# PSUM banks of an expert stage: gate and up sums in a ring of three, all transposes in another ring of three

## The chip, the cores and the metric

The kernel runs on one core of a Trainium2 chip. The metric is device time in microseconds for one execution. The median of three runs before the change is 2891.22 us (2885.97 to 2896.53).

## The reference

One layer of a hybrid block (chunked gating, grouped-query attention, a bidirectional gated recurrence, one output projection) is followed by a mixture of 32 experts. Each of the 2048 tokens, 1024 wide, takes two experts. For every block of an expert's rows the stage computes

```
return (jax.nn.silu(xb @ w1[e]) * (xb @ w3[e])) @ w2[e]
```

with w1 and w3 of 1024 x 512 and w2 of 512 x 1024, multiplies by the gate and adds the rows up by token. Everything is fp32.

## The kernel before

The change lies in the expert stage alone, the function `moe` (L1356 to L1602), which takes the last 830 us. Experts are ranked by their number of tokens, each rank has a fixed room (`CAPS`, L37), and the room is cut into blocks of 128 rows, the last one of 64 where the room is odd. That gives 47 blocks: 29 full ones and 18 half ones. The list `seq` takes turns between large, middle and small experts.

**Precision.** fp32 products are made of three matmuls. A value is split into a high part (fp32r, written by ScalarE) and a low part (the rest, written by VectorE), in `split`, whose two instructions have the lines L82 and L85 wherever it is called. The weights are split the same way by `split_next` (L1425 on ScalarE, L1426 on VectorE). `half16` (L1446, GpSimd) makes a 16-bit copy of the high part.

**Weights.** `pump` (L1410) loads one piece of 512 KB by SyncE into one of five staging tiles `wstage`; the piece is split, its staging tile comes free when L1426 has read it, and the next load is issued. Split pieces wait in rings of 15 (w1, w3) and 7 (w2). Where in the program a piece is split is fixed when the program is built: `need` forces the pieces of the next matmuls, and `ahead` adds one for every 5 units of matmul work if the ring has room.

**One turn.** All engines but SyncE run in program order, and turn i emits, in this order: the gather of the rows of block i+2; a quarter of `gate_up(i)`; `hidden(i-1)`; the scatter of block i-2; a second quarter of `gate_up(i)`; `rows(i+1)`; the rest of `gate_up(i)` with its epilogue; `down(i-1)`.

- `rows` (L1456) transposes the gathered rows of a block on TensorE, eight tiles of 128 columns into the PSUM tile `pxt`, and splits it in two pieces s = 0 and 1 of four tiles each: ScalarE copies the high part `xh` (L82), VectorE subtracts (L85).
- `gate_up` (L1508) adds x @ w1 in the PSUM tile `ph1` and x @ w3 in `ph3`. The first matmuls of a block write `ph1` (two in a full block, one in a half one), the next ones `ph3`, and so on in turns. The epilogue of a full block is SiLU of `ph1` on ScalarE (L1533) and the product with `ph3` on VectorE (L1534). A half block keeps its low products in the other 64 partitions, so ScalarE copies (L1526, L1527) and VectorE adds (L1528, L1529) before SiLU (L1530) and the product (L1531).
- `hidden` (L1473) transposes the product into `pat` and splits it; `down` (L1537) multiplies by w2 into `py`.

The PSUM pool `moep` has one buffer of every tile: `pxt` two banks, `pat` one, `ph1` and `ph3` one each, `py` two; seven of eight banks. A tile's next user waits for all readers of the last one.

Of the kernel before, what the change touches and what calls it, by code (L numbers as in the profile page):

```python
# [10 lines left out]
F32 = mybir.dt.float32  # L11
# [5 lines left out]
OP = mybir.AluOpType  # L17
# [4 lines left out]
P = 128  # L22
D = 1024
KT = D // P
# [50 lines left out]
class Kern:  # L75
# [1280 lines left out]
    def moe(self):  # L1356
        nc, tc, a = self.nc, self.tc, self.a
# [9 lines left out]
        with ExitStack() as es:  # L1367
            pool = es.enter_context(tc.tile_pool(name="moe", bufs=2, reuse_waits="tile"))
            ps = es.enter_context(tc.tile_pool(name="moep", bufs=1, space=PSUM, reuse_waits="tile"))
# [60 lines left out]
            def need(r, w, k):  # L1430
                while (r, w, k) not in W:
                    split_next()
                    clock[0] = max(clock[0] - self.PACE, -self.PACE)
                return W[r, w, k]
# [3 lines left out]
            def ahead(t):  # L1438

                clock[0] = min(clock[0] + t, 3 * self.PACE)  # L1440
                while clock[0] >= self.PACE and dq and free[kind(dq[0][0][1])] > 0:
                    split_next()
                    clock[0] -= self.PACE

            def half16(o, x):
                nc.gpsimd.tensor_scalar(o, x, -65504.0, 65504.0, op0=OP.max, op1=OP.min)  # L1446
# [9 lines left out]
            def rows(i):  # L1456

                n = 64 if half(*seq[i]) else P
                xg = XG.pop(i)
                pt = ps.tile([P, KT, n], F32, name="pxt")  # L1460
                for k in range(KT):
                    nc.tensor.transpose(pt[:, k], xg[:n, k * P:(k + 1) * P], self.ident[:n, :n])
                x = []
                for s in range(2):
                    h = pool.tile([P, 4, P], F32R, name="xh", bufs=4)
                    l = h[:, :, 64:] if n == 64 else pool.tile([P, 4, P], F32R, name="xl", bufs=4)
                    b = pool.tile([P, 4, P], F16, name="xb", bufs=4)
                    self.split(h[:, :, :n], l, pt[:, 4 * s:4 * s + 4])
                    half16(b[:, :, :n], h[:, :, :n])
                    x.append((h, l, b))  # L1470
                XT[i] = x

            def hidden(i):  # L1473

                n = 64 if half(*seq[i]) else P
                ac = AC.pop(i)
                pt = ps.tile([P, 4, n], F32, name="pat")
                for k in range(4):
                    nc.tensor.transpose(pt[:, k], ac[:n, k * P:(k + 1) * P], self.ident[:n, :n])
                h = pool.tile([P, 4, P], F32R, name="ah", bufs=1)  # L1480
                l = h[:, :, 64:] if n == 64 else pool.tile([P, 4, P], F32R, name="al", bufs=1)
                b = pool.tile([P, 4, P], F16, name="ab", bufs=1)
                self.split(h[:, :, :n], l, pt)
                half16(b[:, :, :n], h[:, :, :n])
                AT[i] = [(h, l, b)]

            def mm(i, out, x, ws, cs, last):


                small = half(*seq[i])  # L1490
                first = small and (cs[0] // 2) % 2 == 1
                for low in ((True, False) if first else (False, True)):
                    for m, c in enumerate(cs):
                        h, l, b = (v[:, c % 4] for v in x[c // 4])
                        for s in range(2):
                            w = ws[s][m][low]
                            if not low:
                                nc.tensor.matmul(out[s], h, w, start=(c == 0), stop=(first and c == last))  # L1498
                                if not small:
                                    nc.tensor.matmul(out[s], l, w, start=False, stop=False)  # L1500
                            elif small:
                                z = slice(64 * s, 64 * s + 64)
                                nc.tensor.matmul(out[s][z], b[:, :64], w, start=False, stop=False,
                                                 tile_position=(0, 64 * s))
                            else:
                                nc.tensor.matmul(out[s], b, w, start=False, stop=(c == last))

            def gate_up(i):  # L1508

                r, j = seq[i]  # L1510
                x = XT.pop(i)
                p1 = ps.tile([P, 512], F32, name="ph1")
                p3 = ps.tile([P, 512], F32, name="ph3")
                for kk in range(4):
                    pcs = [need(r, w, kk) for w in ("w1", "w3")]
                    ws = [[[v[:, k * 512:(k + 1) * 512] for v in pc] for k in range(2)] for pc in pcs]
                    mm(i, (p1, p3), x, ws, (2 * kk, 2 * kk + 1), KT - 1)
                    if j == nb(r) - 1:
                        free["w13"] += 2
                    ahead(6.5 if half(r, j) else 12)  # L1520
                    yield
                sg = pool.tile([P, 512], F32, name="sg", bufs=1)
                ac = AC[i] = pool.tile([P, 512], F32, name="ac", bufs=1)
                if half(r, j):
                    z = slice(0, 64)
                    nc.scalar.activation(sg[z], p1[64:], AF.Copy)  # L1526
                    nc.scalar.activation(ac[z], p3[64:], AF.Copy)  # L1527
                    nc.vector.tensor_tensor(sg[z], p1[z], sg[z], op=OP.add)  # L1528
                    nc.vector.tensor_tensor(ac[z], p3[z], ac[z], op=OP.add)  # L1529
                    nc.scalar.activation(sg[z], sg[z], AF.Silu, scale=1.0 / UP)  # L1530
                    nc.vector.scalar_tensor_tensor(ac[z], ac[z], 1.0 / UP, sg[z], op0=OP.mult, op1=OP.mult)  # L1531
                else:
                    nc.scalar.activation(sg, p1, AF.Silu, scale=1.0 / UP)  # L1533
                    nc.vector.scalar_tensor_tensor(ac, p3, 1.0 / UP, sg, op0=OP.mult, op1=OP.mult)  # L1534
                yield
# [37 lines left out]
            with tc.manual_schedule(engines=ENGINES):  # L1573
                for i in range(4):
                    fetch(i)
                for _ in range(self.STG):
                    pump()
                gather(0)
                gather(1)
                rows(0)  # L1580
                for i in range(N):
                    fetch(i + 4)
                    if i + 2 < N:
                        gather(i + 2)
                    g = gate_up(i)
                    next(g)
                    if i:
                        hidden(i - 1)

                    if i > 1:  # L1590
                        scatter(i - 2)
                    next(g)
                    if i + 1 < N:
                        rows(i + 1)
                    for _ in g:
                        pass
                    if i:
                        down(i - 1)
                hidden(N - 1)
                scatter(N - 2)  # L1600
                down(N - 1)
                scatter(N - 1)  # L1602
# [154 lines left out]
```

## Time and profile before

| What | Value |
|---|---|
| Median of three runs | 2891.22 us |
| The profiled execution: its own time, its span | 2883.17 us, 2881.5 us |
| Busy over the span: TensorE, VectorE, GpSimd, ScalarE | 2583.3, 2034.3, 1740.4, 1602.0 us |
| Moved by DMA in the whole program | 410.01 MB, mean 142 GB/s |
| Loads of expert weights | 384 of 512 KB each |

Times are microseconds from the span's start. PE is TensorE, ACT ScalarE, DVE VectorE, POOL GpSimd, SP SyncE. "[1.41 <-DVE xl L85]" behind an instruction in a timeline says that its engine was idle for 1.41 us before it and what ended that. Durations of matmuls overlap: they are pipelined, and the distance of their starts is the time that one takes.

### The profile page before, as it was taken

The numbers are of one execution on the slowest core, as the hardware profiler recorded it, in microseconds if no ns is written. First come the engines' busy times: TensorE is split into PE (matmuls) and PEld (weight loads), VectorE is DVE, ScalarE is ACT, GpSimd is POOL, SyncE is SP. The second block draws the span as 40 slices with busy tenths as digits, with TensorE's granted clock in tenths as the row PEclk, the third lists the DMA queues.
The fourth block names the chain that finished last, engine by engine and source line by source line (L and its number), as shares of the span: only waits on it lengthen the run. The fifth ranks groups of instructions, "written<-read, shape, count | busy, mean of one in ns | idle before, by whom it ended". The sixth has DMA issues, their size and how long they took to land. (4 is left out here: it accounts for less than half of the span.)

```text
span 2881.5 us, 39891 instructions
## 1 busy us (share of the span) xinstructions
PE 2583.3 (90%) x13276; PEld 1904.5 (66%) x13276; DVE 2034.3 (71%) x3049; ACT 1602.0 (56%) x2695; POOL 1740.4 (60%) x1374
## 2 busy tenths in 40 slices
PE   6888898679977999999999999899599999998886
PEld 3788887668865666666666676777366666654553
DVE  3787877674445667667777763778578888888886
ACT  3555554312223777777888774222366666666664
POOL 3335333547774778778888886555455765555553
PEclk9999999789997999999999999999699999999998
DMA  7221223233321111111110005442599999999996
GB/s 284 100 79 63 92 81 106 58 94 99 103 83 50 62 60 59 61 59 40 32 32 31 14 13 172 133 153 99 187 291 298 292 294 312 315 308 299 310 301 171
DMA packets 208688, 410.01 MB, mean 142 GB/s; under 512 B 27568, under 2 KB 82224, under 8 KB 208352
## 3 DMA queue, kind: packets, MB, share of 16 engines
q1 hardware_dynamic: 194976, 367.52, 37.7%
q0 software_dynamic: 13504, 39.93, 6.4%
q8 instruction: 105, 1.72, 0.2%
q14 instruction: 103, 0.84, 0.1%
HBM read 336.00 MB, written 71.37 MB: 141 GB/s over the span
## 5 line engine op out<-in xcount | busy, mean ns | idle before, releaser
L972 POOL TENSOR_TENSOR pl<-pf,ph 128x512 f16<-128x512 f32 x512 | 683.6, 1344 | 156.0 <-ACT ph L969 131.0
L909 DVE TENSOR_REDUCE mx<-pmx 128x1 f32<-128x512 f32 (+1 forms) x640 | 403.3, 635 | 206.8 <-PE pmx L907 199.9
L968 ACT ACTIVATE pf<-s 128x512 f32<-128x512 f32 x576 | 344.3, 598 | 178.5 <-PE s L965 162.4
L1426 DVE SCALAR_TENSOR_TENSOR w13l<-wstage,w13h 128x1024 f16<-128x1024 f32 x256 | 317.8, 1277 | 40.2 <-ACT w13h L1425 37.0
L969 ACT ACTIVATE ph<-s 128x512 fp32r<-128x512 f32 x576 | 342.4, 594 | 0.0
L1498 PE MATMUL ph<-w13h,xh 128*128 128x512 f32 x752 | 291.1, 433 | 48.4 <-DVE sg L1528 25.0
L985 PE MATMUL p<-ph,one 128*128 128x512 f32 x576 | 333.1, 578 | 0.0
L1425 ACT ACTIVATE w13h<-wstage 128x1024 fp32r<-128x1024 f32 x256 | 259.5, 1051 | 108.6 <-DMA wstage<-in_w_dram 81.3
L1446 POOL TENSOR_SCALAR ab<-ah 128x512 f16<-128x512 f32 (+1 forms) x47 | 107.3, 2282 | 312.4 <-ACT ah L82 310.3
L907 PE MATMUL pmx<-k,q 128*128 128x512 f32 (+1 forms) x640 | 242.2, 379 | 8.8 <-DVE mx L909 3.9
L965 PE MATMUL s<-qB,kB 65*128 65x512 f32 x576 | 231.6, 402 | 6.4 <-POOL kB L956 6.4
L964 PE MATMUL s<-q,k 128*128 128x512 f32 x576 | 230.2, 400 | 0.0
L983 PE MATMUL p<-ph,VV 128*128 128x512 f32 x576 | 226.9, 394 | 0.0
L984 PE MATMUL p<-pl,V 128*128 128x512 f16 x576 | 224.2, 389 | 1.1 <-ACT ec L993 1.1
L1498 PEld LDWEIGHTS ph<-w13h,xh 128*128 128x128 f32 x752 | 139.8, 192 | 113.1 <-DVE sg L1528 32.9
L1446 POOL TENSOR_SCALAR xb<-xh 128x512 f16<-128x512 f32 (+1 forms) x94 | 190.7, 2260 | 19.8 <-ACT xh L82 19.5
L1500 PE MATMUL ph<-w13h,xl 128*128 128x512 f32 x464 | 187.3, 404 | 0.0
L1426 DVE SCALAR_TENSOR_TENSOR w2l<-wstage,w2h 128x1024 f16<-128x1024 f32 x128 | 157.1, 1254 | 28.7 <-ACT w2h L1425 23.1
L1425 ACT ACTIVATE w2h<-wstage 128x1024 fp32r<-128x1024 f32 x128 | 132.1, 1053 | 42.3 <-DMA wstage<-in_w_dram 39.5
L984 PEld LDWEIGHTS <-V 128*128 128x128 f16 x576 | 54.9, 95 | 149.7 <-issue 139.2
L1498 PE MATMUL py<-w2h,ah 128*128 128x512 f32 x376 | 146.3, 436 | 7.7 <-DVE ah L85 4.7
L907 PEld LDWEIGHTS pmx<-k,q 128*128 128x128 f32 x640 | 122.4, 191 | 39.8 <-DVE mx L909 10.9
(386 smaller groups left out, 6602.4 us busy)
## 6 DMA issues: line engine op xcount, KB each, us to landing
wstage<-in_w_dram SPq DMA_DIRECT2D x384, 512.0 KB
wm<-in_w_mod_dram SPq DMA_DIRECT2D x48, 512.0 KB
xtok<-in_x_tok_dram SPq DMA_DIRECT2D x34, 512.0 KB
hf<-h_d SPq DMA_DIRECT2D x19, 512.0 KB
xT<-in_xT_dram SPq DMA_DIRECT2D x18, 512.0 KB
h_d<-xT SPq DMA_DIRECT2D x18, 512.0 KB
qf<-qT_d SPq DMA_DIRECT2D x64, 128.0 KB
out_dram<-xn SPq DMA_DIRECT2D x16, 512.0 KB
```

The lines of the kernel that those rows point to most:

```text
L907: nc.tensor.matmul(pm[:, :m], q2[:, t * P:(t + 1) * P], kk[:, j * 512:j * 512 + m], start=True, stop=True)
L909: nc.vector.tensor_reduce(mx[:, t, j:j + 1], pm[:, :m], axis=AX.X, op=OP.max)
L965: nc.tensor.matmul(s, kB[:, g, j], qB, start=False, stop=True)
L968: nc.scalar.activation(pf, s, AF.Exp, scale=0.125)
L969: nc.scalar.activation(ph, s, AF.Exp, scale=0.125)
L972: subs.append(lambda: e.tensor_tensor(pl, pf, ph, op=OP.subtract))
L984: nc.tensor.matmul(p[1], V1[:, g, j].rearrange("p s d -> p (s d)"), pl, **f)
L985: nc.tensor.matmul(p[1], one, ph, start=False, stop=(j == NT - 1))
L1425: nc.scalar.activation(h, st, AF.Copy, scale=UP)
L1426: nc.vector.scalar_tensor_tensor(l, st, UP, h, op0=OP.mult, op1=OP.subtract)
L1446: nc.gpsimd.tensor_scalar(o, x, -65504.0, 65504.0, op0=OP.max, op1=OP.min)
L1498: nc.tensor.matmul(out[s], h, w, start=(c == 0), stop=(first and c == last))
```

## The change

The pieces of `rows` become two tiles of one bank each, `pxt` and `pat` share a ring of three banks, and `ph1` and `ph3` share another, so a block takes two of three. With `py` the stage has eight banks. In the epilogue of a half block two lines on different engines change places.

```diff
-                pt = ps.tile([P, KT, n], F32, name="pxt")
-                for k in range(KT):
-                    nc.tensor.transpose(pt[:, k], xg[:n, k * P:(k + 1) * P], self.ident[:n, :n])
+                pts = []
+                for s in range(2):
+                    pt = ps.tile([P, 4, n], F32, name="pxt", tag="pt", bufs=3)
+                    for k in range(4 * s, 4 * s + 4):
+                        nc.tensor.transpose(pt[:, k - 4 * s], xg[:n, k * P:(k + 1) * P], self.ident[:n, :n])
+                    pts.append(pt)
                 x = []
-                for s in range(2):
+                for pt in pts:
...
-                    self.split(h[:, :, :n], l, pt[:, 4 * s:4 * s + 4])
+                    self.split(h[:, :, :n], l, pt)
...
-                pt = ps.tile([P, 4, n], F32, name="pat")
+                pt = ps.tile([P, 4, n], F32, name="pat", tag="pt", bufs=3)
...
-                p1 = ps.tile([P, 512], F32, name="ph1")
-                p3 = ps.tile([P, 512], F32, name="ph3")
+
+                p1 = ps.tile([P, 512], F32, name="ph1", tag="ph", bufs=3)
+                p3 = ps.tile([P, 512], F32, name="ph3", tag="ph", bufs=3)
...
                     nc.scalar.activation(sg[z], p1[64:], AF.Copy)
+                    nc.vector.tensor_tensor(sg[z], p1[z], sg[z], op=OP.add)
                     nc.scalar.activation(ac[z], p3[64:], AF.Copy)
-                    nc.vector.tensor_tensor(sg[z], p1[z], sg[z], op=OP.add)
                     nc.vector.tensor_tensor(ac[z], p3[z], ac[z], op=OP.add)
```

## Rows read from the trace of the kernel before

**Rows 1.** Busy time by stretch: us, busy per engine (instructions), PEclk, DMA share, GB/s.

```profile
2100.00:2400.00 300.00, 292.48 (x1438) 187.27 (x1436) 251.02 (x253) 189.98 (x236) 188.18 (x109) 1.00 0.93 296
2400.00:2800.00 400.00, 357.70 (x1657) 222.18 (x1656) 334.96 (x333) 256.32 (x310) 216.76 (x130) 0.95 0.97 309
2500.00:2600.00 100.00, 91.44 (x434) 58.55 (x432) 81.93 (x83) 62.38 (x75) 58.35 (x37) 0.98 0.98 308
2600.00:2700.00 100.00, 88.94 (x419) 53.84 (x417) 85.40 (x86) 65.65 (x81) 56.03 (x35) 0.95 0.96 299
```

**Rows 2.** Waits of ScalarE, 2055 to 2881.5: total us, times, longest us.

```profile
ACT w13h L1425 <- DMA wstage<-in_w_dram: 81.3, 71, 4.8
ACT xh L82 <- DVE xl L85: 53.8, 29, 3.6
...
ACT xh L82 <- DVE xh L85: 32.5, 18, 2.9
...
ACT w13h L1425 <- PE ph L1498: 15.3, 6, 5.1
```

**Rows 3.** Waits of TensorE, 2100 to 2400.

```profile
PE ph L1498 <- DVE sg L1528: 5.9, 3, 2.3
```

**Rows 4.** Waits of TensorE, 2400 to 2850.

```profile
PE ph L1498 <- DVE sg L1528: 19.1, 9, 2.7
PE ph L1498 <- ACT sg L1533: 12.7, 6, 3.9
...
PE ph L1498 <- DVE ac L1534: 4.3, 6, 1.1
```

**Rows 5.** Timeline of ScalarE, 2211 to 2223: start, us, engine, line, what.

```profile
2213.44 0.58 ACT L82 ACTIVATE xh<-pxt 128x512 fp32r<-128x512 f32 x1
2215.43 0.60 ACT L82 ACTIVATE xh<-pxt 128x512 fp32r<-128x512 f32 x1 [1.41 <-DVE xl L85]
2215.92 2.94 ACT L1425 ACTIVATE w13h<-wstage 128x1024 fp32r<-128x1024 f32 x3
2218.88 0.59 ACT L1526 ACTIVATE sg<-ph 64x512 f32<-64x512 f32 x1
```

**Rows 6.** Timeline of VectorE, the same stretch.

```profile
2214.71 0.68 DVE L85 TENSOR_TENSOR xl<-pxt,xh 128x512 fp32r<-128x512 f32 x1
2216.05 0.69 DVE L85 TENSOR_TENSOR xl<-pxt,xh 128x512 fp32r<-128x512 f32 x1 [0.66 <-ACT xh L82]
2217.00 3.50 DVE L1426 SCALAR_TENSOR_TENSOR w13l<-wstage,w13h 128x1024 f16<-128x1024 f32 x3 [0.26 <-ACT w13h L1425]
2220.43 0.67 DVE L1528 TENSOR_TENSOR sg<-ph,sg 64x512 f32<-64x512 f32 x1
```

**Rows 7.** Timeline of TensorE, 2217 to 2223.

```profile
2217.68 0.39 PE L1500 MATMUL py<-w2h,al 128*128 128x512 f32 x1
2217.91 1.04 PE L1506 MATMUL py<-w2l,ab 128*128 128x512 f16 x4
2221.16 0.50 PE L1498 MATMUL ph<-w13h,xh 128*128 128x512 f32 x1 [2.21 <-DVE sg L1528]
```

**Rows 8.** Timeline of ScalarE, 2053 to 2071, the second pieces of blocks 0 and 1.

```profile
2058.25 0.60 ACT L82 ACTIVATE xh<-pxt 128x512 fp32r<-128x512 f32 x1 [0.76 <-DVE xl L85]
...
2069.32 0.60 ACT L82 ACTIVATE xh<-pxt 128x512 fp32r<-128x512 f32 x1 [0.76 <-DVE xl L85]
```

**Rows 9.** Timeline of TensorE, 2053 to 2072, the start of the stage.

```profile
2054.89 1.97 PE L1462 MATMUL pxt<-ident,xg 128*128 128x128 f32 x8 [10.94 <-DMA xg<-h_d,idx]
...
2070.91 0.50 PE L1498 MATMUL ph<-w13h,xh 128*128 128x512 f32 x1 [2.52 <-ACT w13h L1425]
```

**Rows 10.** Timeline of TensorE, 2842 to 2846.5, ahead of the last block.

```profile
2845.88 1.09 PE L1498 MATMUL ph<-w13h,xh 128*128 128x512 f32 x2 [2.11 <-DVE sg L1528]
```

**Rows 11.** Timeline of TensorE and VectorE, 2396 to 2405: transposes and the last reader of `pat`.

```profile
2396.32 0.60 PE L1479 MATMUL pat<-ident,ac 128*128 128x128 f32 x4
...
2399.47 1.04 PE L1462 MATMUL pxt<-ident,xg 128*128 128x128 f32 x8
...
2404.01 0.68 DVE L85 TENSOR_TENSOR al<-pat,ah 128x512 fp32r<-128x512 f32 x1
```

## The prediction

> **What bounds the kernel now.** I read the busy times by stretch first, then the waits of ScalarE and TensorE, then the timelines around one block's end. The expert stage has two parts. From 2100 to 2400 TensorE is busy for 292.48 of 300 us while the DMA engines have a share of 0.93: TensorE sets the pace. From 2400 to 2800 TensorE is busy for 357.70 of 400 us only, and the DMA share is 0.97, in the best hundred 0.98, at 309 and 308 GB/s: the weight loads set it [rows 1]. The order of the blocks explains it, since the experts with several blocks per set of weights come early. ScalarE says the same in its waits: 81.3 us in all for pieces that had not landed, and 15.3 us for TensorE to give back a slot of the w1/w3 ring [rows 2].
>
> Two waits concern the change. ScalarE's second copy out of `pxt` waits for VectorE's first subtraction out of `pxt`, in all 29 full blocks (53.8 us) and all 18 half ones (32.5 us) [rows 2]. And TensorE, at the start of `gate_up`, waits until the last block's `ph1` has been read: 5.9 us in three waits before 2400 [rows 3]; after 2400 19.1 us behind half blocks and 12.7 us behind full ones, with 4.3 us more for `ph3` [rows 4].
>
> **The change part by part.** It adds and removes no arithmetic instruction and no DMA; the same 376 row transposes go to PSUM. What it moves are waits.
>
> *Two tiles for the pieces of `rows`.* Around 2213 the two copies and the two subtractions go in turns. ScalarE idles for 1.41 us before its second copy [rows 5]; VectorE then idles for 0.66 us before its second subtraction, and for 0.26 us more until the first weight split behind it is ready [rows 6]. With separate tiles ScalarE goes straight on, and neither gap has a cause left. Queued behind them are three weight splits on each engine and then the readers of `ph1`, L1526 and L1528, which start at 2218.88 and 2220.43 with no idle time before them. So ScalarE reaches L1526 1.41 us earlier and VectorE reaches L1528 0.66 + 0.26 = 0.92 us earlier, at 2219.51. VectorE is the later of the two, and its 0.92 us is what counts.
>
> Is it really the tile that joins the two copies? In half blocks both pieces lie in one bank; in full blocks they are 2 KB apart, so in two banks, and the wait is there in 29 of 29 all the same [rows 2]. Nothing else is common to the two instructions, so I take it that the tile is guarded as a whole. The Trainium skill (PSUM — Partial Sum Buffer, section "PSUM bank collisions raise a hardware error") has instructions of different engines kept apart by bank and quadrant, and lets ScalarE and VectorE work in parallel where they don't collide; by that the full blocks' wait needs another cause than the bank, which the split would not have to remove. The sum by the one reading follows here, by the other under the rivals.
>
> *Three banks for `ph1` and `ph3`.* Block i+1's first sum takes the bank of block i-1's second one, long free. Its second sum takes the bank of block i's first one, and so still waits for L1533 or L1528, but not for the reader of `ph3`. TensorE may start early by the matmuls into the first sum: matmuls start 0.23 us apart [rows 7], so 2 x 0.23 = 0.46 us ahead of a full block and 0.23 us ahead of a half one. At 2221 the wait of 2.21 us [rows 7] becomes 2.21 - 0.92 - 0.46 = 0.83 us, or less, as VectorE also starts its first weight split sooner than the gap says. I take 1.5 us as the relief per wait. The three waits before 2400 have 5.9 us; 3 x 1.5 = 4.5 us go.
>
> *The early part* is bound by TensorE, so these 4.5 us are on the path. Bounds: the early start alone, 3 x 0.46 = 1.4 us, and the whole 5.9 us.
>
> *The start.* In blocks 0 and 1 ScalarE's 0.76 us [rows 8] stands directly before weight splits for which TensorE then waits (2.52 us at block 1 [rows 9]), so 2 x 0.76 = 1.5 us go. Bounds 0 and 1.5.
>
> *The late part* waits for loads, so TensorE's waits there are covered: a faster start of `gate_up` meets ScalarE queued behind a piece that has not landed. What is left is to keep the DMA engines fuller, since a staging tile that comes free 0.92 us sooner is reloaded sooner. If 2400 to 2800 rose from 0.97 to the 0.98 of its best hundred, that would be 0.01 x 400 = 4 us; the hundred with 0.96 and 299 GB/s shows that there are slack moments [rows 1]. Bounds 0 and 4, or the rival below; I take 2.
>
> *The end.* Ahead of the last block TensorE waits for 2.11 us [rows 10] while hardly any load is left to cover it. The last block is a half one: 0.92 + 0.23 = 1.2 us go. Bounds 0.2 and 2.1.
>
> *The ring of transposes.* Each turn takes three tiles in the order `pat`, first piece, second piece, from three banks. Each tile so comes back to the bank it had one turn before, as in the old layout: cost zero. What hides a wait is that the last reader is a turn old; without that, see the third rival. *The eighth bank* may have been another stage's; the first transposes wait 10.94 us for their gather anyway [rows 9]. *The exchanged lines* sit on different engines, whose own orders do not change: zero.
>
> Sum: 1.5 + 4.5 + 2 + 1.2 = 9.2 us. The profiled execution took 2883.17 us, 8 us under the median of the runs and under their lowest; against it the forecast is 2874. Against the median of 2891.22 it is 2882, and that is what I predict.
>
> **The rivals.** *The loads do not bind the late part.* Then its waits on `ph1` and `ph3` are worth what they show, 19.1 + 12.7 + 4.3 = 36.1 us [rows 4], of which 1.5 in 2.2, some 24 us, would go in place of the 2 and the end's 1.2: 30 us in all, 2861. For it: TensorE waits in that part for sums, never for weights, by its own rows [rows 4]. Against it: a DMA share of 0.97 and more [rows 1], and ScalarE's waits for landings, which are what makes the sums' readers late. The Trainium skill (Perfetto Trace Analysis, section "Roofline") puts the ceiling of one core's 16 DMA engines near 435 GB/s, so by it the loads would have room at 309 GB/s; the trace's share says that at this packet mix the engines have none.
>
> *The full blocks' copies still wait.* Then, where full rows are loaded, only the early start is left: 1.4 in the early part, nothing at the start, 0.5 late, 1.2 at the end, whose rows are a half block: 3 us, 2888. For it: two banks and yet a wait.
>
> *The ring joins what was apart.* If a piece of `rows` lands in the bank that `pat` has just used, its transposes wait for VectorE's subtraction out of `pat`, which ends at 2404.69 where the transposes began at 2399.47 [rows 11]: 5 us per block. It decides as soon as a turn's tiles do not come back to their own banks. The early part has 19 of the 47 blocks, 19 x 5 = 95 us with nothing to hide them; the late part has 23, 115 us, of which TensorE's idle 42 us [rows 1] could hide a part: 2891 + 95 + 73 = about 3060. Against it: three tiles a turn in three banks.
>
> **How the numbers follow.** Forecast 0.6, its own range 2878 to 2886 from the bounds above; loads not binding 0.12; full blocks still waiting 0.2; ring 0.04; the rest 0.04, spread. A measurement of this kernel can tell about 0.3% from no change, 8.7 us. The forecast lies just over that line: 0.35 faster, 0.25 same. With the first rival that makes 0.47 faster; with the second and half of the rest 0.47 same; 0.06 slower. The range: 2873 to 2893 for forecast and second rival with some 5 us for runs that differ, as the three do; downward to 2866, part of the way to the first rival; up to 2895. The ring and most of the first rival are left out.
>
> **What would show it.** In the changed profile: no wait of the second `xh` copy for VectorE, and none of the second subtraction for ScalarE beyond a few tenths; the waits of TensorE before 2400 down to about 1.4 us; those after 2400 lower, too, with the total hardly changed by them; DMA share there 0.97 to 0.98. Wrong would be: an unchanged ping-pong, a late part over 10 us shorter, or any wait of the transposes for VectorE.

## The result and the profile after

Four runs of the changed kernel have a median of 2863.96 us (2862.32 to 2867.13), four of the kernel before one of 2893.28 us (2885.97 to 2896.53). The ratio is 0.9913, with a 95% interval of 0.9895 to 0.9931: 25 us faster, where 9.2 were forecast. Against the 2891.22 us that the prediction started from, the ratio makes 2866 us: the lower edge of the range, and well under the 2878 to 2886 us that the forecast's own terms gave.

The profiled execution after took 2865.31 us with a span of 2863.7, some 18 us less than that of before, which was faster than all four of those runs. To see where the time went I mark four places in both traces: the first row transposes, and the starts of the sums of blocks 2, 21 and 45, each after a `down`. Timeline of TensorE, kernel before, the three starts (the first transposes stand in [rows 9]):

```profile
2094.64 0.58 PE L1498 MATMUL ph<-w13h,xh 128*128 128x512 f32 x1
...
2393.62 0.39 PE L1498 MATMUL ph<-w13h,xh 128*128 128x512 f32 x1
...
2829.81 1.08 PE L1498 MATMUL ph<-w13h,xh 128*128 128x512 f32 x4
```

The same places in the changed kernel, with the first transposes:

```profile
2056.20 1.97 PE L1464 MATMUL pxt<-ident,xg 128*128 128x128 f32 x8 [9.91 <-DMA xg<-h_d,idx]
...
2095.35 0.58 PE L1501 MATMUL ph<-w13h,xh 128*128 128x512 f32 x1
...
2390.57 0.39 PE L1501 MATMUL ph<-w13h,xh 128*128 128x512 f32 x1
...
2814.76 1.08 PE L1501 MATMUL ph<-w13h,xh 128*128 128x512 f32 x4
```

The differences of neighbouring marks, and from the last one to the span's end:

| Stretch | before, us | after, us | gained | forecast |
|---|---|---|---|---|
| Start, to block 2 | 39.8 | 39.2 | 0.6 | 1.5 |
| Early part, to block 21 | 299.0 | 295.2 | 3.8 | 4.5 |
| Late part, to block 45 | 436.2 | 424.2 | 12.0 | 2 |
| End | 51.7 | 48.9 | 2.8 | 1.2 |

The late part is far off; the end lies 0.7 us outside its bounds of 0.2 to 2.1 us. The late part from mark to mark, before and after:

```profile
2393.62:2829.81 436.19, 389.58 (x1801) 241.75 (x1800) 367.84 (x364) 281.55 (x341) 235.79 (x142) 0.95 0.97 306
```

```profile
2390.57:2814.76 424.19, 380.32 (x1801) 239.30 (x1800) 369.02 (x364) 281.25 (x340) 244.11 (x142) 0.96 0.98 316
```

The work is the same in both. The time is 2.8% shorter, and the rate of the transfers 3.3% higher. The busy times by stretch, answering to [rows 1]:

```profile
2100.00:2400.00 300.00, 294.48 (x1455) 190.31 (x1454) 258.17 (x257) 192.75 (x239) 195.17 (x110) 1.00 0.94 300
2400.00:2800.00 400.00, 356.34 (x1683) 223.93 (x1682) 346.99 (x344) 263.37 (x320) 232.68 (x135) 0.96 0.98 315
```

Late, the DMA share rose by 0.01 as the 2 to 4 us assumed, but the rate went from 309 to 315 GB/s, by 2%, with the share hardly telling of it.

Now the local mechanism. ScalarE and VectorE around the same block as in [rows 5, 6], first ScalarE:

```profile
2211.33 1.07 ACT L82 ACTIVATE xh<-pxt 128x512 fp32r<-128x512 f32 x2
2213.11 1.06 ACT L1425 ACTIVATE w13h<-wstage 128x1024 fp32r<-128x1024 f32 x1 [0.71 <-DMA wstage<-in_w_dram]
2215.94 2.23 ACT L1425 ACTIVATE w13h<-wstage 128x1024 fp32r<-128x1024 f32 x2 [1.77 <-DMA wstage<-in_w_dram]
2218.20 0.59 ACT L1530 ACTIVATE sg<-ph 64x512 f32<-64x512 f32 x1
```

Then VectorE:

```profile
2214.22 1.27 DVE L85 TENSOR_TENSOR xl<-pxt,xh 128x512 fp32r<-128x512 f32 x2
2215.42 1.20 DVE L1426 SCALAR_TENSOR_TENSOR w13l<-wstage,w13h 128x1024 f16<-128x1024 f32 x1
2217.03 2.39 DVE L1426 SCALAR_TENSOR_TENSOR w13l<-wstage,w13h 128x1024 f16<-128x1024 f32 x2 [0.41 <-ACT w13h L1425]
2219.35 0.68 DVE L1531 TENSOR_TENSOR sg<-ph,sg 64x512 f32<-64x512 f32 x1
```

Both copies run back to back, and so do both subtractions. But ScalarE does not reach the readers of the sums sooner: from its first copy to L1530 it takes 6.87 us, where it took 5.44 us to L1526 [rows 5], since it now waits 0.71 + 1.77 us for pieces that have not landed. VectorE takes 5.13 us from its first subtraction to L1531, where it took 5.72 us to L1528 [rows 6]: 0.59 us less, not 0.92. TensorE at the same place, and all its waits on the sums from 2100 to 2400:

```profile
2218.84 0.40 PE L1503 MATMUL ph<-w13h,xl 128*128 128x512 f32 x1
2220.08 0.50 PE L1501 MATMUL ph<-w13h,xh 128*128 128x512 f32 x1 [0.83 <-DVE sg L1531]
```

```profile
PE ph L1501 <- DVE sg L1531: 3.2, 3, 2.0
```

TensorE starts the first sum at once and waits only before the second, for 0.83 us: to the hundredth what the prediction worked out for this block, though the way there was another, as e1 and e2 show below. The three waits together fell from 5.9 to 3.2 us [rows 3].

ScalarE's waits over the whole stage, answering to [rows 2]:

```profile
ACT w13h L1425 <- DMA wstage<-in_w_dram: 110.7, 90, 4.2
...
ACT sg L1534 <- DVE sg L1531: 39.2, 18, 4.2
...
ACT w13h L1425 <- PE ph L1501: 18.3, 6, 5.8
```

The 86 us of waiting between the copies and the subtractions are gone, in full and in half blocks alike. In their place ScalarE waits 29 us longer for landings of w1/w3 pieces (81.3 to 110.7), and 12.6 us longer for VectorE in the epilogue of half blocks, where it was before:

```profile
ACT sg L1530 <- DVE sg L1528: 26.6, 18, 2.0
```

TensorE's waits from 2400 to 2850, answering to [rows 4]:

```profile
PE py L1501 <- ACT ah L82: 14.3, 4, 5.6
PE py L1503 <- DVE al L85: 9.6, 6, 2.5
PE ph L1501 <- ACT sg L1537: 9.0, 6, 3.0
PE ph L1501 <- DVE sg L1531: 7.9, 6, 1.8
```

Before, the first two of these were, in the other order:

```profile
PE py L1500 <- DVE al L85: 7.3, 4, 2.8
...
PE py L1498 <- ACT ah L82: 3.0, 2, 2.1
```

The waits on the sums fell from 36.1 to 16.9 us, but those on the hidden part grew. All lines of the two views add up to 49.0 us before and 47.7 us after.

### The profile page after: what moved, and what is told of

Same layout as the page of the kernel before. It is cut to its first block, busy times and chain, and to the rows that moved or that the text cites. A ratio compares the mean times of both kernels' runs of the same rounds, so it can differ in the third digit from the quotient of the medians.

```text
span 2863.7 us, 39845 instructions
## 1 busy us (share of the span) xinstructions
PE 2571.5 (90%) x13276; PEld 1902.0 (66%) x13276; DVE 2040.9 (71%) x3049; ACT 1602.6 (56%) x2695; POOL 1756.2 (61%) x1374
## 5 line engine op out<-in xcount | busy, mean ns | idle before, releaser
L1426 DVE SCALAR_TENSOR_TENSOR w13l<-wstage,w13h 128x1024 f16<-128x1024 f32 x256 | 324.4, 1302 | 43.1 <-ACT w13h L1425 39.7
L1425 ACT ACTIVATE w13h<-wstage 128x1024 fp32r<-128x1024 f32 x256 | 262.0, 1052 | 142.6 <-DMA wstage<-in_w_dram 110.7
L1446 POOL TENSOR_SCALAR xb<-xh 128x512 f16<-128x512 f32 (+1 forms) x94 | 213.5, 2651 | 17.4 <-ACT xh L82 17.4
```

Of the source, the lines that this page charges most:

```text
L1425: nc.scalar.activation(h, st, AF.Copy, scale=UP)
L1426: nc.vector.scalar_tensor_tensor(l, st, UP, h, op0=OP.mult, op1=OP.subtract)
```

## The experiments

Two theories stood against each other for the late part. A: it is bound by how soon the staging tiles are refilled, and what holds ScalarE and VectorE up delays that. B: it is bound by TensorE's waits on the sums. D, the prediction's own, has the DMA engines at their ceiling. The stretches below are read at the same four marks, in one execution of each kernel; the ratios rest on 2 (e5, e6, e12) to 12 runs of a kernel.

| Kernel | ratio to before (95%) | start | early | late | end |
|---|---|---|---|---|---|
| before | 1 | 39.8 | 299.0 | 436.2 | 51.7 |
| e1, sums' ring only | 0.9961 (0.9947 to 0.9976) | 38.8 | 299.1 | 432.2 | 50.0 |
| e2, row tiles only | 0.9926 (0.9899 to 0.9952) | 38.0 | 294.9 | 429.2 | 49.0 |
| e3, lines exchanged | 0.9986 (0.9971 to 1.0002) | 41.4 | 302.4 | 436.4 | 50.9 |
| changed | 0.9913 (0.9895 to 0.9931) | 39.2 | 295.2 | 424.2 | 48.9 |
| e4, before, less TensorE work | 0.9915 (0.9888 to 0.9943) | 36.1 | 295.0 | 427.7 | 52.6 |
| e5, changed, less TensorE work | 0.9839 (0.9819 to 0.9858) | 33.7 | 283.6 | 421.0 | 48.9 |
| e6, changed, no low weights | 0.9574 (0.9558 to 0.9591) | 34.6 | 250.8 | 374.8 | 46.2 |
| e7, before, six tiles | 0.9907 (0.9892 to 0.9921) | 39.6 | 299.1 | 409.4 | 50.6 |
| e11, sums' ring, six tiles | 0.9855 (0.9834 to 0.9875) | 39.0 | 299.1 | 402.6 | 49.3 |
| e10, row tiles, six tiles | 0.9825 (0.9805 to 0.9846) | 38.7 | 291.5 | 401.2 | 48.8 |
| e8, changed, six tiles | 0.9800 (0.9785 to 0.9814) | 37.5 | 289.7 | 396.5 | 49.3 |
| e9, changed, seven tiles | 0.9768 (0.9751 to 0.9785) | 36.8 | 289.7 | 385.8 | 49.3 |
| e12, changed, four tiles | 1.0163 (1.0138 to 1.0187) | 41.7 | 315.0 | 470.8 | 54.0 |

How far a stretch can be trusted: the early part is 299.0 or 299.1 us in four kernels with one row tile (before, e1, e7, e11), but 302.4 us in e3, whose total did not change. A difference of some 3 us between two single traces is not shown to come from the edit.

### e1: the ring of the sums alone

```diff
-                p1 = ps.tile([P, 512], F32, name="ph1")
-                p3 = ps.tile([P, 512], F32, name="ph3")
+                p1 = ps.tile([P, 512], F32, name="ph1", tag="ph", bufs=3)
+                p3 = ps.tile([P, 512], F32, name="ph3", tag="ph", bufs=3)
```

> Only the ring of three banks for the gate and up sums; the pieces of the rows stay in one tile. Theory A (the late part is bound by how soon staging tiles are refilled, and the ping-pong between the copies and subtractions out of the row tile delays that): little, 0 to 4 us faster than before, nearly all of it before 2400, the waits of the second copy for VectorE unchanged at some 86 us, late part unchanged within 2 us. Theory B (the late part is bound by TensorE's waits on the sums): 0.46 us for each of some 20 waits after 2400, 8 to 12 us faster, most of it late.

It was 11 us faster, as B had it. By the marks nothing came early (299.0 to 299.1) and 4.0 us late, but the two traces differ by 4.6 us in all, so they do not show where the rest went. Theory A, as put, was wrong here. ScalarE's waits and then TensorE's from 2400 to 2850:

```profile
ACT xh L82 <- DVE xl L85: 55.4, 29, 3.8
...
ACT xh L82 <- DVE xh L85: 31.7, 18, 2.9
```

```profile
PE ph L1498 <- DVE sg L1528: 13.2, 9, 2.4
PE ph L1498 <- ACT sg L1533: 11.2, 6, 2.5
```

The ping-pong (the copies and subtractions out of the row tile, taking turns) is untouched, 87.1 us of it. The waits on the sums are down from 36.1 to 24.4 us [rows 4], but those on the hidden part grew here, too: TensorE's waits in this view add up to 47.3 us, where they were 49.0. Before 2400 the early start gains nothing. TensorE does start the first sum, and then waits as long as before (2.21 us [rows 7]):

```profile
2219.85 0.40 PE L1500 MATMUL ph<-w13h,xl 128*128 128x512 f32 x1
2222.50 0.50 PE L1498 MATMUL ph<-w13h,xh 128*128 128x512 f32 x1 [2.25 <-DVE sg L1528]
```

### e2: the row tiles alone

The changed kernel with the two lines of e1 and the exchanged lines put back.

> Only the two tiles per block of rows with the transposes in a ring of three; the sums keep one bank each and the exchanged lines their old order. Theory A: most of the change, 14 to 22 us faster, the late part (2400 on) 10 us or more of it, DMA rate there up to some 316 GB/s. Theory B: 0.92 us for each wait on the sums, some 28 of them, but only to the extent that TensorE is then on the path: 8 to 14 us; the rest comes with the ring of the sums.

It was 21 us faster, as A had it, though its late part gained 7.0 us by the marks, not 10, and its early part 4.1. TensorE, from 2400 to 2850:

```profile
PE ph L1501 <- ACT sg L1537: 12.2, 6, 3.2
PE ph L1501 <- DVE sg L1532: 9.0, 7, 1.9
...
PE ph L1501 <- DVE ac L1538: 5.6, 6, 1.8
```

The row tiles alone already take 9 us off the waits for the sums (36.1 to 26.8), with one bank for each sum. At the block around 2221 they take off all that the whole change does:

```profile
2223.27 0.50 PE L1501 MATMUL ph<-w13h,xh 128*128 128x512 f32 x1 [0.75 <-DVE sg L1532]
```

Both parts shorten the same waits, one by a later need, the other by an earlier reader. That may be why 11 and 21 us make 25 together and not 32, but the intervals (7 to 15, 14 to 29, 20 to 30) do not show it. Nor do they show that the ring adds to the row tiles: those of e2 and of the changed kernel overlap.

### e3: the exchanged lines alone

```diff
                     nc.scalar.activation(sg[z], p1[64:], AF.Copy)
+                    nc.vector.tensor_tensor(sg[z], p1[z], sg[z], op=OP.add)
                     nc.scalar.activation(ac[z], p3[64:], AF.Copy)
-                    nc.vector.tensor_tensor(sg[z], p1[z], sg[z], op=OP.add)
```

> Only the two exchanged lines in the epilogue of half blocks. Both theories: no change, within 0.2% of before, since each engine's own order stays.

No difference that the interval can tell, 0.9971 to 1.0002.

### e4 and e5: less work for TensorE

```diff
-                                if not small:
-                                    nc.tensor.matmul(out[s], l, w, start=False, stop=False)
```

In e4 in the kernel before:

> The kernel before, without the matmuls of the rows' low part with the weights' high part in full blocks, so TensorE has a third less to do there; loads, splits and copies stay. Theory A: the early part shrinks until loads bind it too (from 300 us to some 270), the late part stays within 4 us of before, its DMA rate at some 309 GB/s. Theory B: the late part shrinks by 15 us or more, too.

In e5 in the changed one:

> The changed kernel, without the matmuls of the rows' low part in full blocks, as in the run of the kernel before without them. Theory A (the late part is bound by refilling the staging tiles): the late part like that of the changed kernel, within 4 us, since TensorE is off its path already. Theory B (TensorE's waits bind the late part): another 8 us or more less from 2400 on.

Busy times of e4, then of e5:

```profile
2100.00:2400.00 300.00, 250.19 (x1157) 141.69 (x1156) 257.85 (x258) 191.28 (x239) 183.75 (x110) 0.92 0.95 302
2400.00:2700.00 300.00, 231.60 (x1026) 128.34 (x1028) 259.72 (x257) 198.13 (x240) 168.44 (x103) 0.88 0.98 318
```

```profile
2100.00:2400.00 300.00, 253.77 (x1196) 145.53 (x1194) 269.85 (x270) 201.87 (x253) 194.95 (x113) 0.94 0.98 320
2400.00:2700.00 300.00, 232.52 (x1033) 130.41 (x1033) 260.46 (x260) 199.05 (x240) 172.60 (x106) 0.89 0.99 318
```

TensorE idles for some 50 us of the early 300 here, although its granted clock there is 0.92 in e4 and 0.94 in e5, where it was 1.00 (a mean over its two levels, 2.4 and 1.2 GHz), so that part of the relief is lost. In the changed kernel the early part falls from 295.2 to 283.6 us, so TensorE did bind it, in part; the late part falls by 3.2 us only. That meets A and rules out B for the changed kernel: its late part does not wait for TensorE. In the kernel before it is the other way round: the early part falls by 4.0 us only, so TensorE at 292 of 300 us was not alone there; with less work for it the loads still stay at 302 GB/s, where e5, with the row tiles and the ring of the sums, reaches 320. The ping-pong is the likely cause, as the row tiles shorten the early part by themselves (e2) and the ring does not (e1), but it was not tried with less work for TensorE. And its late part falls by 8.5 us, outside what either theory had said: before the change, TensorE's lateness did count in the late part.

### e6: how fast the loads can go

```diff
-                l = pool.tile([P, 1024], F16, name=tag + "l", bufs=n)
                 nc.scalar.activation(h, st, AF.Copy, scale=UP)
-                nc.vector.scalar_tensor_tensor(l, st, UP, h, op0=OP.mult, op1=OP.subtract)
...
-                for low in ((True, False) if first else (False, True)):
+                for low in (False,):
```

> The changed kernel, without the low part of the weights: no second split on VectorE and no matmul with it, so a staging tile is free as soon as ScalarE has read it. Loads, gathers and scatters stay. If the DMA engines are at their ceiling in the late part (theory D), the last load is issued within 10 us of where the changed kernel issues it, at a DMA share of 0.98 and some 316 to 320 GB/s. If refilling binds (theory A), the rate rises well over that, to 330 GB/s or more, and the last load comes 25 us or more earlier.

```profile
2100.00:2400.00 300.00, 252.71 (x1131) 195.15 (x1130) 96.74 (x132) 222.59 (x275) 177.15 (x126) 0.93 1.04 352
2400.00:2700.00 300.00, 231.50 (x964) 174.32 (x963) 86.54 (x119) 225.47 (x274) 153.91 (x113) 0.88 1.03 358
```

(The rest of the edit only marks other matmuls as the last ones of a sum.) The rates are 352 and 358 GB/s, with the same five staging tiles, the same gathers and the same scatters, and the last load goes out 98.5 us earlier (2729.07 us, where it was 2827.60). Theory D is out: at 309 GB/s the DMA engines had room for 16% more. The share of 0.97 did not show it; here it reads 1.03, so a reading of 1 is not a limit. VectorE and TensorE have less to do here as well, so this run says what the transfers can do, and the next four say what held them back.

### e7, e8, e9 and e12: more and fewer staging tiles

```diff
-    W13, W2R, STG = 15, 7, 5
+    W13, W2R, STG = 15, 7, 6
```

The same line reads `14, 7, 7` in e9 and `15, 7, 4` in e12. The kernel before with six:

> The kernel before with six staging tiles in place of five. Theory A: the sixth tile covers what the ping-pong delays, 8 to 18 us faster, nearly all of it from 2400 on, with the waits of the copies and of TensorE on the sums unchanged. Theories B and D: within 4 us of before.

The changed kernel with six, seven and four:

> The changed kernel with six staging tiles. Theory A: some of the refill delay is left, 2 to 8 us faster than the changed kernel (0.989 to 0.991 of before). Theories B and D: the same as the changed kernel within 3 us.

> The changed kernel with seven staging tiles and, so that it fits, fourteen slots for split w1/w3 pieces in place of fifteen. Theory A (the late part is bound by refilling): another step in the same direction, 5 to 25 us below six tiles (0.972 to 0.978 of before), smaller than the step from five to six, since VectorE is at 0.92 there. If something else binds by now (TensorE early, VectorE late), or the lost slot costs as much: within 5 us of six tiles.

> The changed kernel with four staging tiles. Theory A: the time from a load's issue to the next use of its tile (some 9.8 us for five tiles, 5 x 1.96 us) is spread over fewer tiles: 2.2 to 2.4 us per piece in the late part, 60 to 110 us slower than the changed kernel over the stage. Theory D (the DMA engines are at their ceiling): within 10 us of it.

Busy times from 2400 to 2700, in this order: the changed kernel with its five, e7, e8, e9, e12.

```profile
2400.00:2700.00 300.00, 274.39 (x1302) 174.25 (x1301) 261.61 (x257) 197.20 (x239) 172.50 (x101) 0.97 0.98 318
```

```profile
2400.00:2700.00 300.00, 285.86 (x1355) 181.52 (x1354) 265.00 (x268) 204.99 (x250) 175.36 (x105) 0.97 0.99 331
```

```profile
2400.00:2700.00 300.00, 285.94 (x1374) 182.08 (x1373) 275.83 (x276) 211.38 (x257) 186.43 (x111) 0.98 1.01 340
```

```profile
2400.00:2700.00 300.00, 290.19 (x1411) 186.25 (x1410) 280.88 (x282) 215.61 (x264) 215.24 (x113) 0.99 1.02 351
```

```profile
2400.00:2700.00 300.00, 256.08 (x1169) 161.28 (x1167) 231.80 (x227) 181.46 (x215) 151.15 (x90) 0.94 0.92 284
```

In the kernel before, the sixth tile leaves the early part alone (299.1) and takes 26.8 us off the late one: refilling bound it. The changed kernel follows the number of tiles at every step: 284, 318 and 340 GB/s with four, five and six, and with seven 351, near the 358 of e6. A had the sign right in all four, and the size for four tiles (72 us slower than with five, where 60 to 110 were expected) and for seven. It had the sizes too small for six tiles (27 us where 8 to 18 were expected, and 33 where 2 to 8 were), and one thing wrong: that the sixth tile would cover the ping-pong. ScalarE in e7:

```profile
ACT xh L82 <- DVE xl L85: 68.7, 29, 4.2
ACT xh L82 <- DVE xh L85: 46.8, 18, 4.6
```

The ping-pong even grows, from 86 to 115 us, and the change is worth 0.9800 against 0.9907, 31 us, with six tiles: no less than with five.

The step from six to seven, which also takes one slot from the split w1/w3 pieces, is 9 us in all, 10.7 in the late part; the intervals of the two just touch. There TensorE is busy for 290 of 300 us and VectorE for 281, so little room is left. e9 is the fastest of the kernels that do all the work, 2820.84 us in the median, 2.3% below before.

### e10 and e11: the two parts with six tiles

e2 and e1 with `STG` of 6.

> The two row tiles and the ring of transposes with six staging tiles, the sums with one bank each. If TensorE's waits on the sums count by holding up ScalarE and VectorE, and with them the refill, they count the more the faster the loads come: 8 to 15 us slower than the changed kernel with six tiles (0.983 to 0.985 of before). If the sums' ring is covered: within 4 us of it.

> The ring of the sums alone with six staging tiles, the row pieces in one tile. If the ping-pong and the waits on the sums are two delays of one loop, this stands between the kernel before with six tiles (0.991) and the changed one with six (0.980): 0.986 to 0.988. If six tiles cover the ping-pong: within 4 us of the changed kernel with six tiles.

| | one bank per sum | ring of the sums |
|---|---|---|
| five tiles, rows in one tile | 1 | 0.9961 |
| five tiles, two row tiles | 0.9926 | 0.9913 |
| six tiles, rows in one tile | 0.9907 | 0.9855 |
| six tiles, two row tiles | 0.9825 | 0.9800 |

e11 lies between its neighbours as two delays in one loop should, 0.0005 below the values expected. The sums' ring is worth 0.0039 and 0.0052 without the row tiles, 0.0013 and 0.0025 with them. The last two are not clear of noise, as the intervals overlap; the larger, some 7 us, is also less than the 8 to 15 us expected of e10.

## Why the prediction was right or wrong

*Direction.* Right: the waits that the two parts remove were named, and they are the ones that went.

*Two tiles for the pieces.* Right. Both gaps have gone in all 47 blocks (what is left is at most 0.26 us, in block 0), so it was the tile that joined the copies: in full blocks the two pieces lay in two banks before and do so now. The rival is out that the full blocks' wait has a cause which the split leaves. The page that raised it, the Trainium skill (PSUM — Partial Sum Buffer, "PSUM bank collisions raise a hardware error"), is not contradicted: in block 0 the trace has VectorE's first subtraction and ScalarE's second copy, out of two banks, at the same time.

```profile
2057.98 0.69 DVE L85 TENSOR_TENSOR xl<-pxt,xh 128x512 fp32r<-128x512 f32 x1 [5.60 <-ACT xh L82]
...
2058.21 0.60 ACT L82 ACTIVATE xh<-pxt 128x512 fp32r<-128x512 f32 x1 [0.26 <-PE pxt L1464]
```

The size was not right: the 0.92 us assumed that ScalarE's time won would reach the readers, and ScalarE spent it on landings.

*Three banks for the sums.* Right in kind: TensorE starts the first sum while the old one is still being read. The 0.46 us that this was to gain at each wait before 2400 did not show: in e1 the wait stood behind the early start at its old length. That 0.92 + 0.46 us gave the 0.83 us of the changed kernel is in part luck, since the row tiles alone gave 0.75.

*The early part.* 4.5 us forecast, 3.8 found. Its reason was only half right. The three waits lost 2.7 us, not 4.5, and e4, with a third less work for TensorE in full blocks, is no shorter here than e2, so TensorE did not set the pace alone.

*The start.* 1.5 us forecast, 0.6 found. The first sum does start 1.35 us sooner after the first transposes (at 2059.80 - 2056.20 = 3.60 us, where it was 2059.84 - 2054.89 = 4.95), and TensorE's wait at block 1 falls from 2.52 to 1.21 us. By block 2 0.6 us of this is left: ScalarE waits for landings there in both kernels, and in the execution after the loads began 1.05 us later against the first transposes (at 2047.82 - 2056.20, where it was 2045.46 - 2054.89).

*The late part.* This step failed: "what is left is to keep the DMA engines fuller", bounded by 4 us from a DMA share of 0.97 against 0.98, with 2 us taken. It measured 12.0 us, and "a late part over 10 us shorter" was one of the prediction's own signs of being wrong. The share was read as a ceiling; e6 moves 16% more through the same engines. What bound the late part was the round of a staging tile: load, split on ScalarE, split on VectorE, next load. Every wait ahead of those splits in the two engines' queues was a wait of the loads, and so were TensorE's waits where ScalarE and VectorE waited for TensorE in turn: without touching the ping-pong the ring takes 4.0 us off the late part with five tiles (e1) and 6.8 us with six (e11 against e7), and e4 takes off 8.5 us. The last link of that chain is argued from these runs, not tried by itself. Nor was TensorE's clock: its granted share in the late part went from 0.95 to 0.96, which could be worth some 4 us (an estimate, 0.01 of 436 us) if TensorE set the pace there. In the changed kernel it does not: e5 has its late part 3.2 us shorter at a clock of 0.89 from 2400 to 2700. For the kernel before no run separates the two.

*The end.* 1.2 us forecast, 2.8 found, of which the 2.11 us ahead of the last block [rows 10] are gone altogether: the sums of the last block start right behind a `down`, and run on.

```profile
2827.68 1.04 PE L1509 MATMUL py<-w2l,ab 128*128 128x512 f16 x4
2828.37 1.63 PE L1501 MATMUL ph<-w13h,xh 128*128 128x512 f32 x4
```

*The rivals.* "The loads do not bind the late part" came out at nearly the right time, 30 us. Half of it holds: the DMA engines were not at their ceiling. Its price did not: it had TensorE's waits on the sums count in full, and in the kernel before a third less matmul work in full blocks gives 8.5 us late (e4), while a sixth staging tile gives 26.8 (e7). The Trainium skill's ceiling of about 435 GB/s (Perfetto Trace Analysis, "Roofline") was named beside that rival; the trace agrees that there was room at 309 GB/s, and shows 358 GB/s as the highest of the 300 us stretches read here. The ring of transposes cost nothing, as forecast: no wait of the transposes for VectorE's subtraction shows up in the changed kernel. (Three waits of 2.1 us in all are for VectorE's product, which the transposes into `pat` read.)

*The other signs.* TensorE's waits before 2400 were to fall to 1.4 us, and fell to 3.2. Those on the sums after 2400 were to fall with the total hardly changed, and did: 36.1 to 16.9, and 49.0 to 47.7 us in all.

*The sum.* 19.2 us by the marks, 25 us by the runs, with an interval of 20 to 30; the profiled execution of before was faster than its four runs, which accounts for the difference in direction, if not to the microsecond. That 2866 us lies on the edge of the stated range is luck: the range went that far only to make room for part of the first rival, whose price did not hold. The terms themselves gave 9.2 us, well under half of what was found.

## What to carry to other kernels

A DMA share near 1 did not mean here that no more would fit (309 GB/s at 0.97, 358 at 1.03): compare the rate with the best that a stripped version of the same stage reaches, or add one buffer, before covering a wait with "the loads bind". Where a load waits for a buffer that two in-order engines must first release, any wait ahead of that release in either queue is a wait of the loads, even on engines that are 64% and 84% busy. A PSUM tile that two engines read piece by piece is worth splitting into a tile for each piece, even where the pieces lie in different banks: in this program that removed 86 us of waits of one engine for the other.

## What the runs showed of the hardware

From 2400 to 2700, going from four to seven staging tiles, and so at most as many loads of 512 KB in flight, raised the rate from 284 to 318, 340 and 351 GB/s, while the DMA share went from 0.92 to 0.98, 1.01 and 1.02: the rate rose by 24%, the share by 11%. Each further tile was worth less than the one before, with one slot for split pieces fewer at seven. With five tiles 358 GB/s were reached in e6, where a tile needs no second split before it is given back.
